# Moving the on-chip pools around layer 1's queries, keys and values, and context's values to the end, in a two-layer diffusion backbone

## The chip, the cores and the metric

One Trainium2 chip, one core of it. The metric is the device time of one execution in microseconds (us), for the whole kernel; the median of several runs counts. The kernel is written in Python against a tile framework that fixes, when the program is built, the order of the instructions in the queue of each engine: TensorE (PE, matmuls; PEld are its weight loads), VectorE (DVE), ScalarE (ACT), GpSimd (POOL) and SyncE (SP), from whose queue every transfer of this kernel is issued.

## What is computed

1024 latent tokens and 256 context tokens of 1024 channels go through two layers; the latent stream is the output. Layer 0 mixes with a recurrent block and a Fourier block, layer 1 with neighbourhood attention in which latent queries also read all context keys. Each layer ends with a gated feed-forward block, and every sub-layer is normalised, shifted, scaled and gated by vectors made from the conditioning (`w_mod`, `b_mod`). Cut to what matters here:

```python
for l in range(DEPTH):                      # DEPTH = 2
    mx = c_act @ w_mod[l] + b_mod[l]        # six vectors for latent tokens; mc: the same for context
    hx, hc = modulate(rmsnorm(x)), modulate(rmsnorm(ctx))
    yx, yc = _ab_mixer(hx, hc, ...) if l == 0 else _na_mixer(hx, hc, ...)
    x = x + gt1 * rmsnorm(yx)
    x = x + gt2 * rmsnorm((silu(fx @ wg) * (fx @ wu)) @ wd)     # fx = modulate(rmsnorm(x)), hidden 2816
    # layer 0 does the same for ctx

def _na_mixer(hx, hc, w_qkv, rpb, w_out, need_ctx):             # 16 heads of 64 channels
    q, k, v = split(hx @ w_qkv);  kc, vc = the same of hc @ w_qkv
    # each query: an 8 x 16 window of keys with a learned bias, and all 256 context keys, in one softmax
    o = softmax([q @ k_window + bias, q @ kc]) @ [v_window, vc]
    return o @ w_out
```

## The kernel before

All arithmetic is float32. TensorE works on pieces: a matrix is split into a high and a low part (ScalarE copies the high part, L326, VectorE subtracts for the low one, L327), and each product is three matmuls (L360, L361, L362). Most products of 512 by 512 blocks are done in a scheme with seven instead of eight block products; hence names as S1 to S4 for sums of weights, T1 to T4 for sums of input blocks, B11, B21, B22 for plain input blocks.

The stages in the order of the run: the mixer of layer 0 (to 345 us), its output product `out_proj0`, the feed-forward's first half `ffn_up` (to about 1060), its down product `ffn_down` (to about 1420), layer 1's values `values_of` (to about 1545), `queries_and_keys` (to 1728), `attention` (to 2008), its output product `out_proj1`, and layer 1's feed-forward (to the end).

**Memory.** Tiles come from pools. A pool is a stretch of the bytes of each partition, opened from the left end or from the right end as a stack, with a number of buffers for each name. Where a new pool lies over the bytes of a closed one, an instruction that writes the new pool is placed in its queue behind the last use of the whole old pool, so the layout decides how early a transfer can be issued. The pools that matter here: `raws` (weights as loaded), `units` (28 split pieces of 4 KB, both right), `hrow` (rows of the hidden layer, left, over ffn_up's pools), `y`, `x` and `v` (left), `uq` (the weights of queries and keys, left, over `v` with its two store buffers `vo`), `qt` (the buffers in which queries and keys are stored), `cxq` (context's split pieces, right), and attention's `q0`, `b0` (head 0's queries and bias, left, over `uq`), `k0` (head 0's keys, right, over `raws`), `qd`, `kd`, `bias`, `s`, `ot`, `vd`, `pt` (left).

**The down product.** `ffn_down` (L1207) goes over the hidden rows in two blocks: four latent token tiles and the context first, four latent tiles then. For each hidden row it loads down weights (L346), stored hidden values h (L1210, 512 KB for two rows) and for context c (L1216, 512 KB for four), splits them, and issues the matmuls. Between the rows it runs fillers: in block 0 the steps of layer 1's modulation vectors (`mod_steps_dve`, L435: VectorE multiplies and adds the loaded 256 KB weights, TensorE sums over the partitions), which end in `mod_finish` (L472). That adds the bias to the row (VectorE, L477), transposes it (four on TensorE, L480) and makes the gains. In block 1 the fillers make layer 1's input blocks.

**Values.** `values_of` (L1394) takes the weights in the order of `value_loads` (L1352). It begins with the context tokens' second half of the channels (g, 48 matmuls), then two passes r = 0, 1 with the blocks B11 and B21 and, between them, the context's first half; between the passes `tb.second` makes the rest of the input blocks; then the products T1, T2, B22, T3, T4. A result goes through `put` (L1406 ScalarE, L1407 VectorE, L1408 store) and two buffers `vo`.

**Queries and keys.** `queries_and_keys` runs over eight pairs of heads. `W.load` (L228) loads gate and up weights of a pair (rg, ru, 512 KB each), GpSimd makes the sums S1 to S4 (L198), the parts are split into ga, s1 to s4, up. Results are stored by a `put` of its own (L1477 to L1479), through two buffers `qo`.

**Attention.** For head 0, and one head ahead for the others, keys, queries, bias and every second head the values are loaded (L1577, L1578, L1581, L1582, L1585; the values 1.28 MB at once). Scores are matmuls (L1601, L1607), then a maximum with bias (VectorE, L1626), the exponential (ScalarE, L1632), a normalisation (GpSimd, L1640), transposes (L1656), and the product with the values (L1675).

Of the kernel before, what the change touches and what calls it, by code (L numbers as in the profile page):

```python
# [16 lines left out]
P = 128  # L17
# [13 lines left out]
ORDER = 'qd kd bias s ot vd pt'  # L31
# [65 lines left out]
class Blocks:  # L97
# [7 lines left out]
    def unit(self, name, k):  # L105
        u = self.u[name, k] = self.kern.unit()
        return u
# [67 lines left out]
class Weights:  # L175
# [3 lines left out]
    def __init__(self, kern, l, cx):  # L179
        self.kern, self.l, self.at, self.extra = kern, l, 0 if cx else 512, None  # L180

    def tile(self, tag, n, dt=F32R):
        return self.kern.t(self.kern.uw, [P, 2, n], dt, tag)
# [96 lines left out]
class Kernel:  # L280
# [136 lines left out]
    def mod_steps(self, l, g, pp, tag):  # L417
# [4 lines left out]
        def step(k):  # L422
# [7 lines left out]
            if k == KD - 1:  # L430
                self.mod_finish(l, g, ps, pp, tag)
# [3 lines left out]
    def mod_steps_dve(self, l, g, pp, tag, rows):  # L435
# [30 lines left out]
        def last():  # L466
            sum_up(3)
            self.mod_finish(l, g, st["ps"], pp, tag)

        return [lambda j=j, h=h: step(j, h) for j in range(4) for h in range(2)] + [last]  # L470

    def mod_finish(self, l, g, ps, pp, tag):  # L472
# [4 lines left out]
        nc.vector.tensor_tensor(mr, ps, bias, op=ALU.add)  # L477
        tp = self.t(pp, [P, 4, P], F32, tag)
# [577 lines left out]
    def open_main(self):  # L1056
# [3 lines left out]
        self.units = self.pool("units", bufs=NU, side="right", stack=self.u2)  # L1060

    def open_y(self, nx=0, side="left", ny=4):
# [4 lines left out]
        if nx:  # L1067
            xp = self.pool("x", bufs=nx, side=side, stack=st)
            self.xrow = lambda m: self.t(xp, [P, D], F32, "x")
        else:  # L1070
            self.xrow = lambda m: self.row()

# [134 lines left out]
    def ffn_down(self, l, blocks, hd, src, store, gg, fillers=((), ()), start=(0, 0), every=(1, 1), between=None):  # L1207
        def load(b, i):
            h = self.hunit().bitcast(F32) if b == 0 else self.unit().bitcast(F32)
# [3 lines left out]
        def loadc(i):  # L1213
            h = self.hunit("c", 2).bitcast(F32).rearrange("p q n -> p (q n)")
# [137 lines left out]
    def value_loads(self, unit, s1):  # L1352


        pool = self.nc.gpsimd.tensor_tensor
# [36 lines left out]
        return plain + sums + [lambda k=k: self.wload(src(1, 1, k), unit) for k in range(4)]  # L1392

    def values_of(self, vp, tb, rows, cx):  # L1394
# [5 lines left out]
        p5, p1 = ([self.t(vp, [P, 512], F32, f"{n}{i}") for i in range(4)] for n in ("q", "p"))  # L1400

        def put(m, half, c):
            u = self.t(vp, [P, 2, 512], F32R, "vo", bufs=2).rearrange("p q (z c) -> p (q z) c", c=P)
# [15 lines left out]
        g = banks("g", 2)  # L1419
        for k in range(KD):  # L1420
            mm(g, cx[k], self.ws.take(), k == 0, k == KD - 1)
        for i, m in enumerate(CTX):
            put(m, 1, g[i])
        g = banks("g", 2)
        for r in range(2):
            d = banks("d")
            for k in range(4):
                w = self.ws.take()
# [614 lines left out]
```

## Time and profile before

| | |
|---|---|
| median of three runs | 2784.2 us (2781.65 to 2784.48) |
| profiled execution | 2787.88 us |
| its span, first to last instruction | 2786.1 us |
| mean granted clock of TensorE | 0.973 of full speed |
| VectorE, ScalarE, GpSimd busy | 62%, 45%, 36% |
| moved by transfers | 397.5 MB, 143 GB/s over the span |

The span is what the profile shows, from the first to the last instruction; the profiled execution's own time is 1.8 us longer. In the rows further down a wait is read as "who <- releaser": the engine stood idle until the named instruction, or the landing of the named transfer, released it. "out<-in" are the names of the tiles written and read; "<-DMA" is a transfer. The clock is the share of full speed that TensorE was granted in a stretch, the DMA share the mean busy share of the core's 16 transfer engines. Matmuls overlap, so a matmul of 0.39 us is issued every 0.23 us at full clock.

### The profile page before, as it was taken

The numbers are of one execution on the slowest core, as the hardware profiler recorded it, in microseconds if no ns is written. First come the engines' busy times: TensorE is split into PE (matmuls) and PEld (weight loads), VectorE is DVE, ScalarE is ACT, GpSimd is POOL, SyncE is SP. The second block draws the span as 40 slices with busy tenths as digits, with TensorE's granted clock in tenths as the row PEclk, the third lists the DMA queues.
The fourth block names the chain that finished last, engine by engine and source line by source line (L and its number), as shares of the span: only waits on it lengthen the run. The fifth ranks groups of instructions, "written<-read, shape, count | busy, mean of one in ns | idle before, by whom it ended". The sixth has DMA issues, their size and how long they took to land. (4 is left out here: it accounts for less than half of the span.)

```text
span 2786.1 us, 36246 instructions
## 1 busy us (share of the span) xinstructions
PE 2607.2 (94%) x12770; PEld 2121.6 (76%) x12770; DVE 1715.0 (62%) x2568; ACT 1252.6 (45%) x2237; POOL 998.9 (36%) x868
## 2 busy tenths in 40 slices
PE   7999998899999998899988798899997999999997
PEld 3677577688888886677866686888875888888786
DVE  4665385856443435766567564777767666556966
ACT  3676254422223323334553342788855333333443
POOL 1000024444343430002036332677625555543811
PEclk9999999999999999999999899899999999999999
DMA  7333472233212226877435444877541332335634
GB/s 243 111 107 123 133 249 84 78 104 112 82 61 74 74 71 229 293 249 255 139 117 182 161 160 160 194 169 164 159 144 69 114 114 98 95 114 174 203 102 144
DMA packets 186664, 397.50 MB, mean 143 GB/s; under 512 B 19569, under 2 KB 49905, under 8 KB 184434
## 3 DMA queue, kind: packets, MB, share of 16 engines
q1 hardware_dynamic: 186482, 395.18, 44.3%
q8 instruction: 101, 1.65, 0.3%
q14 instruction: 81, 0.66, 0.1%
HBM read 309.65 MB, written 85.46 MB: 142 GB/s over the span
## 5 line engine op out<-in xcount | busy, mean ns | idle before, releaser
L360 PE MATMUL d<-u,u 128*128 128x512 f32 x768 | 303.8, 398 | 16.3 <-ACT u L326 10.1
L361 PE MATMUL d<-u,u 128*128 128x512 f32 x768 | 305.1, 397 | 5.2 <-DVE u L327 5.2
L362 PE MATMUL d<-u,u 128*128 128x512 f32 x768 | 303.6, 395 | 0.1
L326 ACT ACTIVATE u<-r 128x512 fp32r<-128x512 f32 x241 | 149.6, 627 | 254.4 <-DMA r<-in_w_down_dram 91.9
L327 DVE TENSOR_TENSOR s<-r,s 128x512 fp32r<-128x512 f32 x208 | 163.2, 792 | 155.2 <-ACT s L326 154.2
L260 POOL TENSOR_TENSOR ss<-ss 128x1 f32<-128x1 f32 x36 | 13.7, 380 | 678.1 <-ACT junk L258 677.9
L361 PE MATMUL g<-u,s 128*128 128x512 f32 x624 | 245.1, 393 | 5.1 <-POOL u L172 4.3
L327 DVE TENSOR_TENSOR u<-r,u 128x512 fp32r<-128x512 f32 x241 | 186.5, 781 | 102.5 <-ACT u L326 98.2
L360 PE MATMUL g<-u,s 128*128 128x512 f32 x624 | 244.5, 392 | 2.1 <-ACT u L122 1.9
L362 PE MATMUL g<-u,s 128*128 128x512 f32 x624 | 244.3, 392 | 0.0
L326 ACT ACTIVATE s<-r 128x512 fp32r<-128x512 f32 x208 | 127.3, 629 | 250.5 <-PE g L362 153.4
L198 POOL TENSOR_TENSOR r<-rg,ru 128x512 f32<-128x512 f32 x52 | 72.7, 1398 | 388.4 <-DMA rg<-in_w_gu_dram 132.4
L360 PEld LDWEIGHTS d<-u,u 128*128 128x128 f32 x768 | 146.4, 191 | 57.7 <-ACT u L326 15.2
L360 PE MATMUL d<-u,ga 128*128 128x512 f32 x416 | 165.7, 398 | 14.2 <-ACT ga L326 14.2
L1640 POOL TENSOR_TENSOR s<-s,sm 128x640 f32<-128x640 f32 (+1 forms) x128 | 151.0, 1200 | 77.7 <-DVE sm L1636 71.2
L361 PEld LDWEIGHTS d<-u,u 128*128 128x128 f32 x768 | 146.6, 191 | 38.8 <-DVE u L327 9.5
L362 PEld LDWEIGHTS d<-u,u 128*128 128x128 f32 x768 | 146.4, 191 | 31.3 <-DVE u L327 1.2
L362 PE MATMUL d<-u,ga 128*128 128x512 f32 x416 | 164.1, 395 | 0.7 <-DVE ga L327 0.6
L361 PE MATMUL d<-u,ga 128*128 128x512 f32 x416 | 164.3, 395 | 0.0
L1168 POOL TENSOR_TENSOR ub<-ub,ua 128x512 f32<-128x512 f32 x44 | 72.8, 1654 | 203.9 <-DVE ua L1167 197.0
L361 PEld LDWEIGHTS g<-u,s 128*128 128x128 f32 x624 | 118.1, 189 | 31.0 <-POOL u L172 5.6
L360 PEld LDWEIGHTS g<-u,s 128*128 128x128 f32 x624 | 117.9, 189 | 28.2 <-ACT u L122 3.5
(453 smaller groups left out, 7002.1 us busy)
## 6 DMA issues: line engine op xcount, KB each, us to landing
mraw<-in_w_mod_dram SPq DMA_DIRECT2D x192, 256.0 KB, 3.8
rg<-in_w_gu_dram SPq DMA_DIRECT2D x44, 512.0 KB, 4.1
ru<-in_w_gu_dram SPq DMA_DIRECT2D x44, 512.0 KB, 3.8
r<-in_w_down_dram SPq DMA_DIRECT2D x88, 256.0 KB, 4.3
x<-x SPq DMA_DIRECT2D x40, 512.0 KB, 4.6
qd<-qd SPq DMA_DIRECT2D x30, 512.0 KB, 11.1
r<-in_w_out_dram SPq DMA_DIRECT2D x48, 256.0 KB, 3.3
h<-hd SPq DMA_DIRECT2D x22, 512.0 KB, 6.3
```

Of the source, the lines that this page charges most:

```text
L198: pool(rs[3], rg[:, h1], ru[:, h1], op=ALU.subtract)
L260: nc.gpsimd.tensor_tensor(st, ss[:, 0:1], ss[:, 1:2], op=ALU.add)
L326: i = nc.scalar.activation(hi, src, AF.Copy) if eng == "act" else nc.vector.tensor_copy(hi, src)
L327: j = nc.vector.tensor_tensor(lo, src, hi.bitcast(F32), op=ALU.subtract)
L360: nc.tensor.matmul(ps, lhs[0], rhs[0], start=start, stop=False)
L361: nc.tensor.matmul(ps, lhs[0], rhs[1], start=False, stop=False)
L362: nc.tensor.matmul(ps, lhs[1], rhs[0], start=False, stop=stop)
L1168: pool(ub, ub, ua, op=add)
L1640: pin(nc.gpsimd.tensor_tensor(s, s, sm.to_broadcast([P, nl + L]), op=ALU.mult))
```

## The change

It lays pools elsewhere, splits one function and moves one piece of work.

- h and c rows of the down product come from `units`; `hrow` is gone. `units` has 20 buffers in layer 0, and 8 more, in a pool `early` to their right, are for the blocks B11 and B21 of layer 1 alone.
- `mod_finish` is split: `mod_row` adds the bias in the step in which it was, the rest is a filler step of its own (30 steps instead of 27; 10 of them in `ffn_up`, 20 in the down product).
- The gain rows get a pool `gg`; `x` is a pool of its own (6 buffers, 4 in block 1; 6 instead of 5 in layer 1's output product). `v` keeps s1, q and p; the store buffers `vo` are a pool on the right; the tiles of `values_of` that were `y` of `v` come from the `y` that stays.
- Context's first half of the values is computed at the end of `values_of`; its eight weight pieces are loaded and split once more.
- `up` of the queries and keys is a pool of its own above `uq`, so that `uq` (rg, ru, ga, s4, s1, s3, s2) lies over `y` and `v` only and `up` over `vo` and part of `v`.
- Attention: `kd`, `qd` and `bias` on the right, over `raws` and `early` only; head 0 uses them as every other head does; `s`, `ot`, `vd`, `pt` on the left, `vd` over `qt` and `cxq`.

```diff
...
-ORDER = 'qd kd bias s ot vd pt'
+ORDER = 'kd qd bias s ot vd pt'
+ASIDE = ("qd", "kd", "bias")
...
     def unit(self, name, k):
-        u = self.u[name, k] = self.kern.unit()
+        kern = self.kern
+        u = self.u[name, k] = kern.first_unit() if name in ("B11", "B21") else kern.unit()
...
     def turned(self, xs, k):
...
     def __init__(self, kern, l, cx):
-        self.kern, self.l, self.at, self.extra = kern, l, 0 if cx else 512, None
+        self.kern, self.l, self.at, self.extra, self.apart = kern, l, 0 if cx else 512, None, {}
     def tile(self, tag, n, dt=F32R):
-        return self.kern.t(self.kern.uw, [P, 2, n], dt, tag)
+        return self.kern.t(self.apart.get(tag, self.kern.uw), [P, 2, n], dt, tag)
     def load(self, f):
...
-                self.mod_finish(l, g, ps, pp, tag)
+                self.mod_finish(l, g, self.mod_row(l, g, ps), pp, tag)
...
         def last():
...
-            self.mod_finish(l, g, st["ps"], pp, tag)
-        return [lambda j=j, h=h: step(j, h) for j in range(4) for h in range(2)] + [last]
-    def mod_finish(self, l, g, ps, pp, tag):
+            st["mr"] = self.mod_row(l, g, st["ps"])
+        return ([lambda j=j, h=h: step(j, h) for j in range(4) for h in range(2)]
+                + [last, lambda: self.mod_finish(l, g, st["mr"], pp, tag)])
+    def mod_row(self, l, g, ps):
...
+        return mr
+    def mod_finish(self, l, g, mr, pp, tag):
+        nc, a = self.nc, self.a
...
-    def open_main(self):
+    def open_main(self, apart):
...
-        self.units = self.pool("units", bufs=NU, side="right", stack=self.u2)
+        self.first_unit = self.unit
+        if apart:
+            early = self.pool("early", bufs=8, side="right", stack=self.u2)
+            self.first_unit = lambda: self.t(early, [P, 2, 512], F32R, "u")
+        self.units = self.pool("units", bufs=NU - 8 * apart, side="right", stack=self.u2)
     def open_y(self, nx=0, side="left", ny=4):
...
-            xp = self.pool("x", bufs=nx, side=side, stack=st)
-            self.xrow = lambda m: self.t(xp, [P, D], F32, "x")
+            self.open_x(nx, side)
...
+    def open_x(self, n, side):
+        self.x_stack = ExitStack()
+        xp = self.pool("x", bufs=n, side=side, stack=self.x_stack)
+        self.xrow = lambda m: self.t(xp, [P, D], F32, "x")
     def load_scale(self, ms, src):
...
     def ffn_down(self, l, blocks, hd, src, store, gg, fillers=((), ()), start=(0, 0), every=(1, 1), between=None):
         def load(b, i):
-            h = self.hunit().bitcast(F32) if b == 0 else self.unit().bitcast(F32)
+            h = self.unit().bitcast(F32)
...
         def loadc(i):
-            h = self.hunit("c", 2).bitcast(F32).rearrange("p q n -> p (q n)")
+            h = self.row()
...
-        return plain + sums + [lambda k=k: self.wload(src(1, 1, k), unit) for k in range(4)]
+        last = [lambda r=r, c=c, k=k: self.wload(src(r, c, k), unit) for r, c in ((1, 1), (0, 0), (1, 0)) for k in range(4)]
+        return plain + sums + last
     def values_of(self, vp, tb, rows, cx):
...
-        p5, p1 = ([self.t(vp, [P, 512], F32, f"{n}{i}") for i in range(4)] for n in ("q", "p"))
+        p5, p1 = ([self.t(vp["v"], [P, 512], F32, f"{n}{i}") for i in range(4)] for n in ("q", "p"))
         def put(m, half, c):
-            u = self.t(vp, [P, 2, 512], F32R, "vo", bufs=2).rearrange("p q (z c) -> p (q z) c", c=P)
+            u = self.t(vp["o"], [P, 2, 512], F32R, "vo").rearrange("p q (z c) -> p (q z) c", c=P)
...
         def banks(tag, n=4):
...
-        g = banks("g", 2)
-        for k in range(KD):
-            mm(g, cx[k], self.ws.take(), k == 0, k == KD - 1)
-        for i, m in enumerate(CTX):
-            put(m, 1, g[i])
-        g = banks("g", 2)
+        def context(c):
+            g = banks("g", 2)
+            for k in range(KD):
+                mm(g, cx[k], self.ws.take(), k == 0, k == KD - 1)
+            for i, m in enumerate(CTX):
+                put(m, c, g[i])
+        context(1)
...
-                w = self.ws.take()
-                mm(d, tb.u[("B11", "B21")[r], k], w, k == 0, k == 3)
-                mm(g, cx[4 * r + k], w, r == 0 and k == 0, r == 1 and k == 3)
+                mm(d, tb.u[("B11", "B21")[r], k], self.ws.take(), k == 0, k == 3)
...
-            c = self.t(vp, [P, 512], F32, "y", bufs=self.ny)
+            c = self.t(self.yp, [P, 512], F32, "y", bufs=self.ny)
...
-        for i, m in enumerate(CTX):
-            put(m, 0, g[i])
         def product(tag, name):
...
-        u4 = [self.t(vp, [P, 512], F32, "y", bufs=self.ny) for _ in range(4)]
+        u4 = [self.t(self.yp, [P, 512], F32, "y", bufs=self.ny) for _ in range(4)]
...
+        context(0)
     def queries_and_keys(self, W, T, cx):
...
-        q0 = self.t(self.pool("q0", side="left", stack=self.kst), [P, 2, T], F32, "q0")
-        b0 = self.t(self.pool("b0", side="left", stack=self.kst), [P, 896], F32, "bi0")
-        k0p = self.pool("k0", side="right", stack=st)
-        be0 = self.t(k0p, [P, 512], F32, "be0")
-        k0 = self.t(k0p, [P, TT], F32, "k0")
...
-        pools = {n: self.pool(n, bufs=size.get(n, 1), side="left", stack=st) for n in ORDER.split()}
+        pools = {n: self.pool(n, bufs=size.get(n, 1), side="right" if n in ASIDE else "left", stack=st) for n in ORDER.split()}
...
-        bint = [b0, self.t(bp, [P, 896], F32, "bi1")]
-        bedge = [be0, self.t(bp, [P, 512], F32, "be1")]
+        bint = [self.t(bp, [P, 896], F32, f"bi{i}") for i in range(2)]
+        bedge = [self.t(bp, [P, 512], F32, f"be{e}") for e in range(2)]
...
-            kt = self.t(kd, [P, TT], F32, "kd") if h else k0
-            qt = self.t(qd, [P, 2, T], F32, "qd") if h else q0
+            kt = self.t(kd, [P, TT], F32, "kd")
+            qt = self.t(qd, [P, 2, T], F32, "qd")
...
-        self.open_main()
+        self.open_main(1)
...
-        self.ffn_up(0, W, tb, hd, cx, mods[:9])
+        self.ffn_up(0, W, tb, hd, cx, mods[:10])
...
-        self.open_y(6, ny=6)
+        self.open_y(0, ny=6)
+        gst = ExitStack()
+        gp = self.pool("gg", side="left", stack=gst)
+        self.open_x(6, "left")
...
-        gg = [self.gain_rows(0, 2, w, self.yp, self.pp, "g") for w in range(2)]
+        gg = [self.gain_rows(0, 2, w, gp, self.pp, "g") for w in range(2)]
...
-        hst = ExitStack()
-        hp = self.pool("hrow", side="left", stack=hst)
-        self.hunit = lambda tag="h", n=3: self.t(hp, [P, 2, 512], F32R, tag, n)
         def between():
-            hst.close()
...
+            self.x_stack.close()
+            self.open_x(4, "left")
...
+            vp["o"] = self.pool("vo", bufs=2, side="right", stack=vst)
         def vrow():
...
-                      (mods[9:], self.turn_steps(tb, rows, x2, cx, vp)), (0, TS), (2, 1), between)
+                      (mods[10:], self.turn_steps(tb, rows, x2, cx, vp)), (0, TS), (2, 1), between)
+        self.x_stack.close()
+        gst.close()
+        self.u_stack = ExitStack()
+        vp["v"] = self.pool("v", side="left", stack=self.u_stack)
+        vrow()
+        self.values_of(vp, tb, rows, cx)
+        self.u_stack.close()
...
-        self.u_stack = ExitStack()
-        vp["v"] = self.yp = self.pool("v", side="left", stack=self.u_stack)
-        vrow()
-        self.t(vp["v"], [P, 512], F32, "y", bufs=self.ny)
-        self.values_of(vp["v"], tb, rows, cx)
-        self.u_stack.close()
...
-        for n in "rg ru ga s4 s1 s3 s2 up".split():
-            self.t(self.uw, [P, 2048 if n in ("ga", "up") else 1024], F32, n)
+        for n in "rg ru ga s4 s1 s3 s2".split():
+            self.t(self.uw, [P, 2048 if n == "ga" else 1024], F32, n)
...
+        W.apart["up"] = self.pool("up", side="left", stack=self.u_stack)
...
-        self.open_main()
-        self.open_y(5, side="right")
+        self.open_main(0)
+        self.open_y(6, side="right")
...
+        self.x_stack.close()
...
```

The loads of a head in attention go in the order keys, queries, bias, values, as before; the arithmetic is the same, instruction for instruction, but for eight more splits of weight pieces.

## Rows read from the trace of the kernel before

**Rows 1.** The page, part 1: busy time of each engine over the span.
```profile
PE 2607.2 (94%) x12770; PEld 2121.6 (76%) x12770; DVE 1715.0 (62%) x2568; ACT 1252.6 (45%) x2237; POOL 998.9 (36%) x868
```

**Rows 2.** Waits of TensorE: in all, how often, the longest, us.
```profile
PE s L1601 <- DMA q<-qd: 16.3, 1, 16.3
...
PE d L360 <- ACT ga L326: 14.2, 1, 14.2
PE d L360 <- ACT u L326: 10.1, 2, 9.1
...
PE g L480 <- DVE mg L477: 7.5, 1, 7.5
```

**Rows 3.** Stretches: length, busy of PE, PEld, DVE, ACT, POOL; clock; DMA share, GB/s.
```profile
1071.00:1090.00 19.00, 19.00 (x78) 15.43 (x77) 13.51 (x26) 8.74 (x19) 0.00 (x0) 0.92 0.91 310
1090.00:1110.00 20.00, 20.00 (x86) 15.62 (x85) 14.89 (x27) 8.54 (x18) 0.00 (x0) 1.00 0.83 269
1148.00:1156.00 8.00, 0.55 (x3) 0.27 (x2) 5.87 (x12) 5.71 (x12) 0.00 (x0) 0.79 1.02 379
1156.00:1180.00 24.00, 24.00 (x101) 19.85 (x101) 17.30 (x33) 9.16 (x24) 0.00 (x0) 0.93 0.85 288
1457.00:1470.00 13.00, 8.08 (x37) 6.13 (x35) 12.73 (x11) 5.87 (x10) 10.92 (x8) 1.00 0.25 82
1535.00:1550.00 15.00, 1.04 (x2) 0.50 (x2) 5.54 (x8) 4.41 (x6) 0.78 (x1) 0.61 0.65 245
1745.00:1759.00 14.00, 10.68 (x49) 9.23 (x48) 6.83 (x19) 6.15 (x14) 5.07 (x5) 0.58 1.04 223
```

**Rows 4.** Time line, SyncE and ScalarE, after ffn_up: start, length, [idle before].
```profile
1062.46 3.50 SPq L1210 DMA_DIRECT2D h<-hd  x3
...
1069.67 0.63 ACT L326 ACTIVATE u<-h 128x512 fp32r<-128x512 f32 x1 [7.15 <-DMA h<-hd]
```

**Rows 5.** Time line, ScalarE and VectorE, in the down product.
```profile
1148.45 0.63 ACT L326 ACTIVATE u<-r 128x512 fp32r<-128x512 f32 x1 [4.46 <-DMA r<-in_w_down_dram]
...
1149.11 0.69 DVE L327 TENSOR_TENSOR u<-r,u 128x512 fp32r<-128x512 f32 x1 [3.41 <-ACT u L326]
...
1155.00 0.68 DVE L477 TENSOR_TENSOR mg<-g,mraw 128x512 f32<-128x512 f32 x1
```

**Rows 6.** Time line, SyncE, ScalarE and TensorE, from values to queries and keys.
```profile
1528.54 14.77 SPq L1408 DMA_DIRECT2D vd<-vo  x8
...
1547.85 1.06 ACT L326 ACTIVATE ga<-rg 128x1024 fp32r<-128x1024 f32 x1 [5.61 <-DMA rg<-in_w_qk_dram]
...
1548.96 0.80 PE L360 MATMUL d<-u,ga 128*128 128x512 f32 x1 [14.22 <-ACT ga L326]
```

**Rows 7.** Time line, SyncE, ScalarE and TensorE, from keys to attention.
```profile
1726.60 0.57 SPq L1585 DMA_DIRECT2D vd<-vd  x1
1728.03 3.42 SPq L1479 DMA_DIRECT2D kd<-qo  x2
...
1738.20 0.61 SPq L1578 DMA_DIRECT2D q<-qd  x1
...
1736.76 0.38 ACT L1477 ACTIVATE qo<-d 128x256 fp32r<-128x256 f32 x1 [6.58 <-DMA kd<-qo]
...
1744.31 0.77 PE L1601 MATMUL s<-k,q 128*128 128x256 f32 x2 [16.32 <-DMA q<-qd]
```

**Rows 8.** Attention by tile and line: ns min/median/max, first to last start.
```profile
L1577 SPq DMA_DIRECT2D k<-kd x2: 505/558/611, 1701.9 to 1707.0; - x2
...
L1675 PE MATMUL o<-pt,vd x704: 274/282/562, 1759.1 to 2007.5; 128*128 128x256 f32 x176
...
L1607 PE MATMUL s<-kd,qd x240: 278/280/416, 1761.2 to 1995.9; 128*128 128x256 f32 x120
```

**Rows 9.** The view of transfers: issues, KB each, median us to landing.
```profile
r<-in_w_out_dram SPq DMA_DIRECT2D x48, 256.0 KB, 3.3
...
vd<-vd SPq DMA_DIRECT2D x8, 1280.0 KB, 9.0
```

## The prediction

> **What bounds the kernel now.** I read the page first: TensorE is busy for 94% of the span [rows 1], so only time in which it stands still, or runs at the lower of its two clock levels, can be had back without less arithmetic; the change removes no arithmetic. Then the waits of TensorE [rows 2]; four long single ones lie where this change works: 16.3 us for the first queries of attention (wait G), 14.2 for the first gate weights of the queries and keys (F), 9.1 for the first split piece of the feed-forward's down product (C) and 7.5 for a modulation row inside it (D). Then the table of stretches [rows 3], for the clock behind each gap and for what else is near its limit. Last the time line around each gap, for what ended it [rows 4 to 7].
>
> C: the first three loads of stored hidden rows (h) are issued at 1062.46, and ScalarE, which splits them, gets the first at 1069.67 [rows 4]. In this kernel a load into a pool stands in SyncE's queue behind the last use of every pool that its own addresses overlap; h rows lie over ffn_up's pools. D: ScalarE gets the next row of down weights 4.46 us late, VectorE stands behind it in order, and so its addition of the modulation row starts at 1155.00 only, while TensorE has that row's transposes next in its queue [rows 5]. F: eight stores of values go out between 1528.54 and 1543.3, the gate weights' load stands behind them, and lands at 1547.85, 4.5 us after its issue; TensorE starts at 1548.96 after 14.22 us [rows 6]. G: head 0's key loads were issued while the keys were still made [rows 8], but its query loads wait for the pool uq and for the stores. A 1.28 MB load of attention's values enters at 1726.60 between those stores, such a load takes 9.0 us to land [rows 9], the store of 1728.03 holds its buffer until ScalarE can go on at 1736.76, the second query load leaves at 1738.20, and TensorE starts at 1744.31 [rows 7].
>
> The profiled execution took 2787.9 us, its span is 2786.1; the median of three runs is 2784.2, 3.7 lower. The sum is made against 2787.9 and the result lowered by the same 3.7. Runs of this kernel can tell 0.2%, 5.6 us, from no change.
>
> **Part 1, h and c rows from the units (C).** The pool hrow goes; its loads now need free units only, and units come free while ffn_up's last products run. So the loads can be issued some 15 us earlier, before its end, and ScalarE's 7.15 us of waiting [rows 4] ends ahead of TensorE's last product. Gain: the wait of 9.1 less 1 to 2 for what must still follow ffn_up's last output (x loads, gain rows), and part of the lower clock behind it: 0.92 over 19 us [rows 3] is 1.5 us lost. I take 9, ends 4 and 11. The price: weights, h and c rows and the first blocks of layer 1 now share 20 units and 8 early ones instead of 28 and a pool of their own; this lowers how far the splits run ahead. In 1090 to 1110 TensorE was busy for 20.00 of 20 us [rows 3]; I take 1 us of loss, ends 0 and 4 (more is rival 3).
>
> **Part 2, mod_finish split (D).** Its addition stays in its step, its four transposes come one filler step later, two hidden rows, some 8 us of matmuls. The addition was over at 1155.7, 7.4 us after TensorE stopped, so it is just in time; what is next in the queue, the products of the rows before, was split long before (only the transposes were waited for; after them 24.00 of 24 us are busy [rows 3]). Gain 7.5, plus a part of the clock (0.93 over 24 us, 1.7 lost): 8, ends 3 and 9, the lower one if ScalarE's late weights, which are what made VectorE late, show up as a wait further on. With the transposes move four copies, up to two small vector operations and, from the second group on, one load (the post-norm gains) on SyncE: all fall in slots where VectorE waited for ScalarE anyway [rows 5], 0. The three added filler steps fit in the slots of block 0.
>
> **Part 3, context's values last, and the pools v, vo, up (F).** The 48 context matmuls of one half, 11.2 us at 20.00/86 us each [rows 3], leave the two passes ahead of the second half of the input blocks and come after the last product. In 1457 to 1470 VectorE is the bound: 12.73 us of 13, TensorE 8.08 [rows 3]. Taking 24 matmuls, 5.6 us, out of the first pass lets VectorE's chain start 5.6 us earlier, and its two context splits of 0.7 us leave it: the last product ends 6.9 earlier. The 11.2 us of context then lie in the 14.22 us that TensorE waits anyway [rows 6], because the gate weights no longer lie over the store buffers: their load needs the last value's arithmetic, not its store. The stores still pace this arithmetic through two buffers, so the load goes out about 6.9 earlier, at 1536.4, lands 4.5 later, and split and start are as before: start at 1542, which is 7 earlier. Off this come 2 us for eight more weight loads of 256 KB (2.1 MB; in 1535 to 1550 the queues moved 245 GB/s at a share of 0.65, so the rest of their capacity, some 130 GB/s, would take it in 16 us: mostly hidden). A shorter gap gives 1 back in the clock. I take 6, ends 0 and 9. The splits of these weights (8 of 0.63 us on ScalarE, 0.69 on VectorE) lie in the time when VectorE is waited for; that is what the lower end holds. Context's two stores move behind all others on SyncE; nobody needs them before attention's values: 0.
> The Trainium skill (DMA: Bandwidth & Descriptors, Anatomy of one DMA) counts about 2 us fixed and the bytes at 436 GB/s for a transfer, fitted on another queue than SyncE's; for these 512 KB that makes an estimate of 3.2 us, where the row has 4.5. By the page the term would be 1.3 larger; the row decides.
>
> **Part 4, attention's pools (G).** kd, qd and bias now lie at the right over raws and the early units only, both done with the second product of the last pair, some 16 us before its end; nothing they load lies over uq. Queries and keys of head 0 are stored by then (its key loads left at 1701.9 and 1707.0 [rows 8]). So both pairs of loads go out near 1711 and land before TensorE's last product at 1728.0. The load of values lies over qt and cx and must now follow the last store, at about 1736 at the latest: it no longer stands between the stores. What remains: the scores follow the last product at once; their first softmax must wait until the splits of the last keys are through VectorE, about 1731.5 without the 6.58 us of ScalarE [rows 7]. The gain is 16.3 less 2 to 3 for this hand-over, plus up to 5.9 for a clock of 0.58 over 14 us [rows 3], of which I take 1 to 2, as a shorter gap also lowers the clock. Against it: the values' load, 9.0 us [rows 9], lands about 1745, and the first matmul with them, at 1759.1 [rows 8], would be due at 1744 to 1745: 0 to 2 lost. I take 15, ends 5 and 22.
>
> **Part 5, the rest.** raws now overlap kd, so the first rows of the output weights are loaded after the last scores at 1995.9 and not before; they land in 3.3 us [rows 9] and are needed at 2008, after twelve us of the last heads' values, which cover them: 0. If the queue were held until then, it would cost those 3.3. A sixth x buffer: 0, by the same cover. The mixer's end and out_proj0 have the same pools but for the cap on units: 0.
>
> **Sum:** 9 + 8 + 6 + 15 − 1 = 37. 2787.9 − 37 = 2750.9 for the execution, 2747 for the median.
>
> **Rivals.** (1) One of the two large waits stays: at F the stores, two at a time, remain what paces the end and the new loads take the queue from them, so F gives 0; or at G the loads are still placed behind the last stores and G gives 5. Then 31 or 27 us: about 2755 (2753 to 2757). For: SyncE issues everything in one order fixed ahead. Against: the only overlaps left are those named.
> (2) What C and D give back is waited for later, since the down product's block 0 is bound by transfers: share 0.83 to 0.85 in 1090 to 1110 and 1156 to 1180, and 1.02 in the gap D itself [rows 3]; the same bytes in 17 us less need a share of about 0.92. Then C and D give 0 to 4 of 17: 2747 + 15 = 2762. Against: TensorE misses nothing at 0.83 to 0.91.
> (3) Slower: the 20 units. Weights, split h, split c and their raw rows all come from one pool in block 0; if the lead falls under what a late load takes (4.46 us in D), TensorE waits at every filler step, some 20 of them. At 37/20 = 1.9 us each the gain is gone; at D's remaining size, 2.2 each, it is 44, and the time 2791. For: share 1.02 in 1148 to 1156. Against: live time per row is two hidden rows only, and 20.00 of 20 us with DMA at 0.83.
> (4) The change doesn't do what it says: a load remains behind an unnamed use (an overlap of v with y's last reader, of kd with a late raw): F and G both give half, C and D all: 2747 + 10 = 2757, inside rival 1's range; counted there.
>
> **Numbers.** Forecast 0.56, rival 1 with 4 0.22, rival 2 0.13, rival 3 0.09. The forecast's own range is 2734 (about all upper ends together, 11 + 9 + 9 + 22 = 51) to 2757, where rival 1 begins. The range to hold 8 of 10 reaches over rivals 1 and 2 with their bounds and leaves rival 3 and the far tail: 2734 to 2770. Faster by over 0.2%: forecast, 1 and most of 2: 0.88; within: rival 3 at about its point of balance, 0.05; slower 0.07.
>
> **What would show it.** C: no wait of TensorE above 2 us between 1055 and 1075, h loads issued before ffn_up's last product. D: no wait for L477's successor. F: context's matmuls after the last product, a wait of some 3 us for the gate weights in place of 14.2. G: loads of qd issued before the last key stores, TensorE's first scores within 2 us of its last product, the values' load last. Wrong: new waits of TensorE for u<-r or u<-h all through block 0, a wait for vd at the first values above 3 us, or a load of rg behind the last store.

## The result and the profile after

The changed kernel takes 2751.4 us in the median of four runs (2747.5 to 2757.0), the kernel before 2782.9 in the runs beside it: a ratio of 0.9892, interval 0.9868 to 0.9915. That is 31.5 us less, where the forecast was 37 (2747). A second measurement of the changed kernel gave 2748.4, ratio 0.9879 (0.9859 to 0.9898). The profiled execution has a span of 2751.6 us, 34.5 shorter than that of before.

The waits of TensorE in the changed kernel, columns as in [rows 2]:

```profile
PE s L1612 <- DVE mx L1637: 22.1, 9, 5.2
...
PE d L363 <- DVE u L329: 11.2, 7, 6.8
PE d L362 <- ACT u L328: 10.7, 2, 9.4
...
PE d L362 <- ACT ga L328: 2.5, 1, 2.5
```

The four waits of [rows 2] answer to this: G's 16.3 us for queries is gone, and the longest wait for a maximum (mx) is 5.2 instead; F's 14.2 is 2.5; C's and D's are gone; in D's place a wait of 3.3 us stands in the down product (below). The 9.4 for a split u looks like C's 9.1 but is another one: it lies in the values, and was not there before.

Where the time went is best read from lengths of stages, each from the first or last matmul of a name in the time line to the next such mark. They add up to TensorE's last matmul.

| us, from mark to mark | before | changed | changed, 2nd time |
|---|---|---|---|
| start to ffn_up's last | 1059.4 | 1059.9 | 1064.8 |
| to the down product's first (C) | 11.0 | 1.9 | 1.9 |
| to the values' first (D lies here) | 333.5 | 330.7 | 324.9 |
| to the first of queries and keys (F) | 145.1 | 140.0 | 141.3 |
| to their last | 179.0 | 178.3 | 178.3 |
| to the first with attention's values (G) | 31.1 | 18.0 | 17.0 |
| to the last of these | 248.7 | 244.2 | 247.0 |
| to TensorE's end | 765.6 | 765.7 | 765.7 |

The first row varies from 1052.7 to 1066.7 over the 14 traces kept here, and that of attention from 240.1 to 249.9. So a total tells no difference under some 5 us, and the experiments are read by the stage. The stages of C, F and G repeat within 1.5 us in the two traces of the changed kernel; the down product does not (330.7 and 324.9, at a clock of 0.98 and 1.00), and its length alone prices nothing under some 6 us.

Stretches of the changed kernel, columns as in [rows 3]:

```profile
1061.00:1071.00 10.00, 10.00 (x45) 7.70 (x42) 5.61 (x11) 6.56 (x14) 0.04 (x1) 1.00 1.00 307
...
1150.00:1166.00 16.00, 12.70 (x53) 10.13 (x52) 11.98 (x24) 6.58 (x18) 0.00 (x0) 0.91 0.96 349
...
1436.00:1457.00 21.00, 5.03 (x11) 3.54 (x12) 20.97 (x19) 10.51 (x18) 15.47 (x11) 0.59 0.21 62
...
1518.00:1533.00 15.00, 11.72 (x49) 8.98 (x49) 7.81 (x13) 6.79 (x11) 0.00 (x0) 0.99 0.84 289
```

The first is where C was: TensorE is busy for all of it, at full clock. The second is in the down product, behind the place of D: TensorE still stands for 3.30 us there, as its time line has it:

```profile
1164.04 0.80 PE L362 MATMUL d<-u,u 128*128 128x512 f32 x1 [3.30 <-DVE y L257]
```

The last is the end of the values, where it worked for 1.04 of 15 us before [rows 3] and now for 11.72, on context. The third is the price: in the second pass of the values TensorE has little to do for 21 us, while VectorE works for 20.97 of them.

The time line of the changed kernel, SyncE at C:

```profile
1044.78 0.63 SPq L1225 DMA_DIRECT2D u<-hd  x1
...
1046.14 1.19 SPq L1225 DMA_DIRECT2D u<-hd  x2
```

The h loads that left at 1062.46 [rows 4] leave 15 us before ffn_up's last matmul (1059.9).

SyncE, ScalarE and TensorE at F:

```profile
1525.50 0.32 SPq L1425 DMA_DIRECT2D vd<-vo  x1
1525.87 1.17 SPq L230 DMA_DIRECT2D rg<-in_w_qk_dram  x1
...
1531.32 1.06 ACT L328 ACTIVATE ga<-rg 128x1024 fp32r<-128x1024 f32 x1 [1.39 <-DMA rg<-in_w_qk_dram]
...
1532.43 0.50 PE L362 MATMUL d<-u,ga 128*128 128x512 f32 x1 [2.45 <-ACT ga L328]
```

The gate weights go out ahead of context's last two stores, not behind all of them as in [rows 6], and their landing lies under context's matmuls but for 2.45 us. The values began 11.4 us earlier; less this, the load leaves 6.1 earlier than before, where the forecast had 6.9.

SyncE, VectorE and TensorE at G:

```profile
1693.84 0.58 SPq L1588 DMA_DIRECT2D kd<-kd  x1
1694.51 0.55 SPq L1589 DMA_DIRECT2D qd<-qd  x1
...
1713.36 2.84 SPq L1495 DMA_DIRECT2D kd<-qo  x2
...
1719.55 0.57 SPq L1596 DMA_DIRECT2D vd<-vd  x1
...
1715.24 0.43 DVE L1494 SCALAR_TENSOR_TENSOR qo<-d,qo 128x256 fp32r<-128x256 f32 x1 [1.91 <-ACT qo L1493]
...
1710.60 0.40 PE L1612 MATMUL s<-kd,qd 128*128 128x256 f32 x2
...
1717.07 1.01 PE L1612 MATMUL s<-kd,qd 128*128 128x384 f32 x2 [5.24 <-DVE mx L1637]
```

The loads of head 0's keys and queries begin 17 us before the last product ends (1710.8); the first scores follow it at once; the values' load goes behind the last stores; and the first softmax waits until VectorE has split the last keys at 1715.24, which is the 5.24 us that stay.

### The profile page after: what moved, and what is told of

Its sections match the earlier page's. It is cut to its first block, busy times and chain, and to the rows that moved or that the text cites. A ratio compares the mean times of both kernels' runs of the same rounds, so it can differ in the third digit from the quotient of the medians.

```text
span 2751.6 us, 36277 instructions
## 1 busy us (share of the span) xinstructions
PE 2603.5 (95%) x12770; PEld 2120.1 (77%) x12770; DVE 1716.0 (62%) x2576; ACT 1257.5 (46%) x2245; POOL 990.2 (36%) x868
## 6 DMA issues: line engine op xcount, KB each, us to landing
qd<-qd SPq DMA_DIRECT2D x32, 512.0 KB, 10.6
```

## The experiments

Each but one is an edit of the changed kernel. Ratios are against the kernel before.

**1. C undone: h and c rows in a pool of their own again.**

```diff
-            h = self.unit().bitcast(F32)
+            h = (self.hunit() if b == 0 else self.unit()).bitcast(F32)
...
-            h = self.row()
+            h = self.hunit("c", 2).bitcast(F32).rearrange("p q n -> p (q n)")
...
+        hp = self.pool("hrow", side="left", stack=hst)
+        self.hunit = lambda tag="h", n=3: self.t(hp, [P, 2, 512], F32R, tag, n)
```

> The changed kernel with h and c rows back in a pool of their own over ffn_up's pools (units stay at 20 and 8). Theory: the place of that pool alone made the wait at the start of the down product, so TensorE's wait there is back at 8 to 9.5 us, and the rest of the stage is as in the changed kernel or 1 to 2 us better; total 6 to 9 us above the changed kernel, about 2759. Rival: the rows' share of the 20 units is what makes the 2.0 and 3.3 us waits left in the changed kernel's down product; then those two vanish and the total is 3 to 4 above it, about 2755.

Measured: 2763.0 us, ratio 0.9929 (0.9907 to 0.9951).

```profile
1065.75 3.08 SPq L1225 DMA_DIRECT2D h<-hd  x3
...
1072.51 0.63 ACT L328 ACTIVATE u<-h 128x512 fp32r<-128x512 f32 x1 [6.72 <-DMA h<-hd]
```

This is the time line of that kernel; it is [rows 4] again, and the stage of C is 10.6 us long against 1.9. The theory holds: the place of the pool made the wait. The rival falls: the down product behind it takes 331.3, not less than the 324.9 to 330.7 of the kernels whose rows share the units; it even has a wait of 6.14. The total lies 11.6 above the changed kernel, where 6 to 9 was expected; 8.7 of it is this stage, and the rest is within the spread of the others.

**2. D: the split of mod_finish, in three ways.** First undone in the changed kernel:

```diff
-            st["mr"] = self.mod_row(l, g, st["ps"])
+            self.mod_finish(l, g, self.mod_row(l, g, st["ps"]), pp, tag)
...
-                + [last, lambda: self.mod_finish(l, g, st["mr"], pp, tag)])
+                + [last])
```

> The changed kernel with mod_finish in one step again (27 filler steps, 9 of them in ffn_up). Theory: the addition of the modulation row stands behind splits that wait for late down weights, so TensorE's wait for the row is back at 5 to 8 us near 1140, but the lead that VectorE and ScalarE regain in it takes away the 3.3 us wait behind it: 2 to 4 us above the changed kernel, about 2754. Rival: the two waits have nothing to do with each other: 7 to 8 above, about 2759.

Measured: 2754.0 us, ratio 0.9893 (0.9869 to 0.9916). TensorE waits for the row again:

```profile
1142.41 1.12 PE L487 MATMUL g<-ident,mg 128*128 128x128 f32 x4 [6.71 <-DVE mg L480]
```

The 3.3 behind it is gone, and the down product takes 330.7 us, as in the first trace with the split. In the second trace with the split it takes 324.9, with waits of 1.5 and 1.0 only, so this run alone doesn't tell what the split is worth; the rival's 7 to 8 us above did not come. Then the split alone, in the kernel before:

> The kernel before with mod_finish split and nothing else. Theory: the wait of 7.5 us for the row goes, but the late down weights behind it then end in waits for split pieces of 4 to 8 us further on in the down product: within 3 us of the kernel before. Rival (the forecast's own step): nothing takes its place, 7 to 8 us below the kernel before.

Measured: 2784.2 us over ten runs, ratio 1.0003 (0.9986 to 1.0020). Its time line, TensorE, and ScalarE ahead of the second wait:

```profile
1153.77 0.66 PE L485 MATMUL g<-ident,mg 128*128 128x128 f32 x4 [1.22 <-DVE mg L478]
1173.01 0.79 PE L360 MATMUL d<-u,u 128*128 128x512 f32 x1 [6.33 <-DVE y L255]
...
1165.60 0.63 ACT L326 ACTIVATE u<-r 128x512 fp32r<-128x512 f32 x1 [6.31 <-DMA r<-in_w_down_dram]
```

The wait of 7.45 us for the row becomes 1.22 and a new one of 6.33, 19 us later. It is for L255, which reads out the banks of the first half of the product so that the second half can use them: ScalarE and VectorE come to it late, as they stand in order behind splits of down weights that land late (the load waited for left at 1158.85, behind modulation loads that took 4.70 and 2.13 us to issue, and took 6.7 us to land). The theory holds, with the place corrected: what came next was the read-out, not a split. Why the weights are late is seen on SyncE in the changed kernel:

```profile
1153.54 6.77 SPq L416 DMA_DIRECT2D mraw<-in_w_mod_dram  x3
1160.40 0.86 SPq L348 DMA_DIRECT2D r<-in_w_down_dram  x2
```

Three modulation loads take 6.77 us to issue, and down weights follow only at 1160.40. If it is a free buffer that the queue stands for (there are three), more buffers cure it:

```diff
-        self.open_mraw()
+        self.open_mraw(14)
```

> The changed kernel with 14 buffers instead of 3 for loaded modulation weights in the down product (in the bytes that the h and c rows left). Theory: the waits of 2.0 and 3.3 us left there come from SyncE's queue, which stands for a buffer of these weights with down weights behind; they vanish, and the values start 4 to 6 us earlier: about 2747. Rival: the transfers themselves are the bound (share 0.85 to 0.96): the loads then come earlier and take the same share, the waits move and stay within 1.5 us of their sum, about 2751; or the loads, ahead of the down weights, make them later: up to 5 us more.

Measured: 2741.5 us, ratio 0.9850 (0.9818 to 0.9881). Stretches of that kernel:

```profile
1066.00:1085.00 19.00, 19.00 (x82) 14.77 (x82) 16.21 (x28) 7.61 (x16) 0.00 (x0) 1.00 1.05 390
...
1145.00:1165.00 20.00, 20.00 (x89) 16.44 (x88) 16.08 (x28) 11.42 (x27) 0.00 (x0) 1.00 0.94 321
```

TensorE is busy throughout both, with shares of 1.05 and 0.94 and 390 GB/s at the highest, and the down product takes 323.5 us. What SyncE's queue stood for between 1065 and 1240 us, columns as in [rows 2], first in the changed kernel:

```profile
SPq L416 <- DMA mraw<-in_w_mod_dram: 40.1, 22, 4.0
```

Then with 14 buffers:

```profile
SPq L416 <- DMA mraw<-in_w_mod_dram: 2.6, 8, 0.3
```

So in the changed kernel the transfers were not the bound; one queue was, which stood for three buffers. With these buffers, and mod_finish in one step:

> The changed kernel with 14 buffers and mod_finish in one step again. Theory: what makes the modulation row late is SyncE's queue standing for a buffer with down weights behind it; with 14 buffers the weights are on time, TensorE waits under 2 us for the row, and the total is within 2 us of the run with 14 buffers and the split. Rival: the addition is late because it stands in order behind splits on VectorE whatever the loads do: a wait of 5 to 7 us, and as much above.

Measured: 2740.1 us, ratio 0.9848 (0.9827 to 0.9869); the down product takes 320.4 us and TensorE has no wait over 0.6 us in block 0. With the buffers the split is worth nothing to be seen: the theory.

**3. F: order and pools apart.** First context's half back in the two passes, pools as changed:

```diff
-                mm(d, tb.u[("B11", "B21")[r], k], self.ws.take(), k == 0, k == 3)
+                w = self.ws.take()
+                mm(d, tb.u[("B11", "B21")[r], k], w, k == 0, k == 3)
+                mm(g, cx[4 * r + k], w, r == 0 and k == 0, r == 1 and k == 3)
...
-        context(0)
```

> The changed kernel with context's half of the values back in the two passes (no extra weight loads), pools as changed. Theory: the pools alone let the gate weights' load go before the last stores, but nothing lies over its landing: the last product ends about 5 us later than in the changed kernel and a wait of 5 to 9 us stands before the first product of queries and keys; total 4 to 7 above the changed kernel, about 2757. Rival: the order does nothing, as the passes are bound by VectorE: the total is within 1.5 us of the changed kernel.

Measured: 2757.5 us, ratio 0.9911 (0.9883 to 0.9939).

```profile
1524.22 0.42 SPq L230 DMA_DIRECT2D rg<-in_w_qk_dram  x1
...
1530.51 0.80 PE L362 MATMUL d<-u,ga 128*128 128x512 f32 x1 [11.37 <-ACT ga L328]
```

The stage of the values takes 143.7 us: of the 5.1 that the changed kernel gains over 145.1 (3.8 in its second trace), the pools alone give 1.4. The theory's total came out, but by chance: the stage is 2.4 to 3.7 longer than in the changed kernel, the wait is 11.37 and not 5 to 9, and attention took 249.9 us, the longest of all. The rival falls by the stage. Then the order alone, by laying `up` back into uq, which so lies over the values' store buffers:

```diff
-        for n in "rg ru ga s4 s1 s3 s2".split():
+        for n in "rg ru ga s4 s1 s3 s2 up".split():
...
-        W.apart["up"] = self.pool("up", side="left", stack=self.u_stack)
```

> The changed kernel with up back in the pool uq, which then lies over the store buffers of the values (attention's pools stay on the right). Theory: attention needs only one of the two moves, so its gap stays at 5 to 7 us (first wait), but the first gate weights stand behind the last store of values, context's stores included: 8 to 12 us more before the first product of queries and keys; total 8 to 12 above the changed kernel, about 2761. Rival: up apart is what lets attention start, whatever its pools: then a wait of 14 to 17 us before its scores as well, about 2772.

Measured: 2751.4 us, ratio 0.9877 (0.9855 to 0.9900). TensorE before queries and keys, and at the second group of scores in attention:

```profile
1529.31 0.80 PE L362 MATMUL d<-u,ga 128*128 128x512 f32 x1 [8.62 <-ACT ga L328]
...
1714.89 1.01 PE L1612 MATMUL s<-kd,qd 128*128 128x384 f32 x2 [5.50 <-DVE mx L1637]
```

The wait before the first product of queries and keys is 8.62 us instead of 2.45, and the stage takes 146.4, no less than before the change. Neither half gives the gain; both together do. (The expected loss of 8 to 12 was 5 to 6 in the stage; the total doesn't show it, the spread of the other stages being as large.) In attention its first wait is 5.50 us, as in the changed kernel.

**4. G: attention's pools undone.**

```diff
+        q0 = self.t(self.pool("q0", side="left", stack=self.kst), [P, 2, T], F32, "q0")
...
-        pools = {n: self.pool(n, bufs=size.get(n, 1), side="right" if n in ASIDE else "left", stack=st) for n in ORDER.split()}
+        pools = {n: self.pool(n, bufs=size.get(n, 1), side="left", stack=st) for n in ORDER.split()}
...
-            kt = self.t(kd, [P, TT], F32, "kd")
-            qt = self.t(qd, [P, 2, T], F32, "qd")
+            kt = self.t(kd, [P, TT], F32, "kd") if h else k0
+            qt = self.t(qd, [P, 2, T], F32, "qd") if h else q0
```

> The changed kernel with attention's pools as before the change (head 0's queries and bias on the left over the queries' and keys' weights, its keys on the right, kd, qd and bias on the left; x with 5 buffers in the output product after it). Theory: the wait of 16 us before the first scores is back, with the load of values between the last stores: 16 to 18 above the changed kernel, about 2768. Rival: most of the gap was the hand-over of the last keys through two store buffers and the softmax, so 8 to 11 above, about 2761.

Measured: 2754.2 us, ratio 0.9897 (0.9873 to 0.9921). Both expectations fall: the first wait is 6.20 us, and the stage of G takes 21.4 against 31.1 before and 18.0 changed. So the layout of attention is worth 3.4 of 13.1, given the rest of the change. A new theory: in this kernel head 0's queries lie over uq again, as before the change; what matters is which work ends last in uq, and with `up` gone from it that work ends before the last two products, which read `up`. Then undoing both must bring the wait back, and `up` alone must not (that was experiment 3's second kernel).

> The changed kernel with both undone: attention's pools as before the change and up in uq. Theory: with the queries of head 0 over a pool that ends with the last product again, the 14 to 17 us before the first scores are back, with the 8 to 12 us before queries and keys: 18 to 28 above the changed kernel, about 2774. Rival: the gap of the kernel before came from the order of the load of values alone, which follows the stores now: a first wait of 6 to 8 us and 10 to 14 above, about 2763.

Measured: 2763.3 us, ratio 0.9920 (0.9898 to 0.9941). The time line of TensorE at the start of attention, first with attention's pools alone undone:

```profile
1715.41 0.77 PE L1617 MATMUL s<-k,q 128*128 128x256 f32 x2 [6.20 <-issue]
```

Then with both undone:

```profile
1723.54 0.77 PE L1617 MATMUL s<-k,q 128*128 128x256 f32 x2 [16.16 <-DMA q<-qd]
```

First waits of 5.24 (neither undone), 5.50 (`up`), 6.20 (attention) and 16.16 (both): either move suffices, and the two don't add. SyncE's queue, again first with attention's pools alone undone:

```profile
1695.84 0.61 SPq L1594 DMA_DIRECT2D q<-qd  x1
...
1709.81 0.61 SPq L1594 DMA_DIRECT2D q<-qd  x1
...
1714.73 0.57 SPq L1601 DMA_DIRECT2D vd<-vd  x1
```

Then with both undone:

```profile
1705.97 0.57 SPq L1601 DMA_DIRECT2D vd<-vd  x1
...
1710.88 0.72 SPq L1594 DMA_DIRECT2D q<-qd  x1
...
1717.99 0.61 SPq L1594 DMA_DIRECT2D q<-qd  x1
```

With both undone the first load of queries leaves 3.5 us after the last product (1707.4) and not 13.4 before it (1709.2), which is what the new theory asks for. But the theory is not the whole of it. With attention's pools alone undone, the first load at 1695.84 left 7.8 us before the last product that reads uq was over (1703.6); so the pool decides the place in SyncE's queue at most, and what sets that place was not followed up. And with both undone the load of values has moved as well, from behind the last stores to between them, as in [rows 7], and the second load of queries leaves only behind the last store of keys (1717.42). So no run here tells the place of the queries from the place of the values, and the rival, whose load of values was to follow the stores, was not put to the test. The total was 11 nearer to the changed kernel than the theory had it; the rival's total came out, by other stages.

**5. A better version.** Beside the 14 buffers, the second pass's weight splits ahead of the input blocks, and a store buffer for the last keys:

```diff
+                self.ws.finish(self.ws.at + 4)
                 tb.second(rows)
...
+            u = self.t(tp, [P, 2, L], F32R, "qc") if n == L else self.t(tp, [P, 2, 512], F32R, "qo", bufs=2)
```

> The 14 buffers, and two more edits of the changed kernel: the four weight splits of the values' second pass are issued before the rest of the input blocks is made, and the last keys (of context) have a store buffer of their own. Theory: T1 starts 2 to 3 us earlier, since that split no longer stands behind the input blocks on ScalarE and VectorE, and attention's first softmax 2 us earlier; with 4 to 6 of the buffers 8 to 11 below the changed kernel, about 2742. Rival: VectorE is busy throughout the stretch before T1, so the place of one split changes nothing there (under 1 us), and the softmax has its next wait in the bias: 4 to 6 below, about 2747.

Measured: 2746.3 us, ratio 0.9858 (0.9837 to 0.9879): the rival's total, and its reason for the values. The waits in the values move behind the pass (8.8 and 6.2 us), since VectorE is the bound there, and the stage takes 138.4 us against 138.7; the first softmax comes 2 us earlier, and the first matmul with attention's values doesn't: 17.7 us against 17.8. Here the rival's reason, the bias, is not what the trace shows:

```profile
1714.05 1.43 PE L1687 MATMUL o<-pt,vd 128*128 128x256 f32 x10 [2.34 <-DMA vd<-vd]
```

That matmul waits for the landing of the values, whose load leaves 8.8 us after the last product (8.1 with the 14 buffers alone); VectorE's wait of 5.33 for a bias comes 4 us later.

> The changed kernel itself once more, so that the runs beside it have it on the same chip: 2748 to 2755 by either theory.

> The changed kernel with 14 buffers for loaded modulation weights and the early split of the second pass's weights, without the store buffer for the last keys. Theory: the buffers give the 5 to 8 us in the down product that their first run showed, and the early split 1 to 2 before queries and keys: 6 to 10 below the changed kernel of this call. Rival: the first run of the buffers was a good draw of attention, whose length differs by up to 10 us between runs of the same code: 3 to 4 below it.

Measured: the changed kernel 2748.4 us (2745.5 to 2755.6); with the buffers and the early split 2742.2, ratio 0.9855 (0.9832 to 0.9879). That is 6.2 below, at the theory's lower edge. The three kernels with 14 buffers but without the store buffer lie at 2740.1 to 2742.2, 6 to 11 under the two measurements of the changed kernel. Their intervals still overlap or touch it; the down product does not: 320.4 to 323.9 us in four traces with them, 324.9 to 331.3 in eight of the changed kernel and its other variants. They are faster than the kernel before, and by that stage and the queue's waits than the changed one, by an amount that the totals leave open; the early split adds nothing to be seen.

## Why the prediction was right, and where it was not

**C, 9 forecast:** 9.1 (11.0 to 1.9) in both traces. The mechanism and the size were as written; the price of 1 us for 20 units did not show.

**D, 8 forecast: the step that failed.** "What is next in the queue ... was split long before" was true, and the wait for the row went. But the cause, ScalarE's late weights, stayed, and in the kernel before 6.3 of 7.45 us came back at the read-out of the first half (3.3 in the changed kernel); alone the split is worth 0 (ratio 1.0003, where 8 us less would be 0.9971). The lower end of 3, "if ScalarE's late weights ... show up as a wait further on", named the mechanism and still put it too high. Rival 2 had the waits move too, but by transfers at their limit; with the queue no longer held up, the same bytes went without a wait at shares of 0.94 and 1.05. Still the down product is 2.8 to 8.6 us shorter in the changed kernel than before, and is 2.8 shorter without the split; what gives this (the clock, which was 0.98 and 1.00 in its two traces and 0.98 before, the first rows' earlier start, or the pools) was not taken apart.

**F, 6 forecast:** 5.1 and 3.8. The load left within 1 us of the time worked out. That the second pass would then wait 16 us for a split behind the input blocks was not foreseen; it costs little because VectorE's work, not TensorE's, sets that stretch. The page named there makes the landing, by estimate, 3.2 us where the row had 4.5 (the Trainium skill, DMA: Bandwidth & Descriptors, Anatomy of one DMA); in the changed kernel it was 5.5 (1525.87 to 1531.32), in a stretch with a DMA share of 0.84 where before it was 0.65 [rows 3]. The measurement is further off the page's figure than before.

**G, 15 forecast:** 13.1 and 14.1 to the first matmul with attention's values, the rest within the spread of attention. The end was right: scores at once, the softmax after the last split (1715.2, forecast 1731.5 less the 17 that came before). The cause was only one of two: "nothing they load lies over uq" is enough, but so is `up` taken out of uq, which the forecast counted for F alone.

**The sum:** 9.1 + 2.8 + 5.1 + 0.7 + 13.1 + 4.5, less 0.5 in the first row, is 34.8 between the trace before and the first of the changed kernel, and the medians have 31.5. Forecast 37; in these two traces D's 2.8 for 8 makes most of the difference. In the second trace the down product is 8.6 shorter and the first row, where nothing was meant to change, 5.4 longer, so that D's share of the total can't be read from two traces; that its step failed is read from the split alone in the kernel before. Rival 1 fell by F and G, rival 3 by the down product's length.

## What to carry to other kernels

Where a pool may be written only behind all of an older pool's work, ask which tile of the older pool is used last: one tile moved out let the loads over the others leave earlier here. A wait that is ended by an engine which itself waited is not cured by giving its waiter other work; follow the releaser back until a queue or a resource comes, here one in-order queue that stood for three buffers. And fill a gap at the end of a stage only together with what starts the next one: the layout gave 1.4 alone and the order nothing, and together they gave 5.1 and 3.8.

## What was not expected of the hardware

VectorE took 0.68 us for the subtraction of L174 when GpSimd was idle, and 1.7 beside GpSimd's work, in the stretch that bounds the values. The time line of the changed kernel, VectorE:

```profile
1434.28 5.12 DVE L174 TENSOR_TENSOR u<-y,u 128x512 fp32r<-128x512 f32 x3
...
1453.91 0.68 DVE L174 TENSOR_TENSOR u<-y,u 128x512 fp32r<-128x512 f32 x1
```

GpSimd, idle for 1.16 us around the second row:

```profile
1454.60 1.73 POOL L1388 TENSOR_TENSOR s<-r,r 128x512 f32<-128x512 f32 x1 [1.16 <-DVE u L174]
```

GpSimd was busy for 15.47 of the 21 us there. The Trainium skill (SBUF — State Buffer, SBUF: two separate sides) says that the two share a port pair which one of them holds for a whole instruction; the rows agree, and no run here took the work off GpSimd. The other surprise is the spread: attention took 240 to 250 us in kernels with the same code for it. Its longest and its shortest, in the kernel of experiment 3 with the order undone and in the one with 14 buffers, columns as in [rows 3]:

```profile
1725.70:1975.60 249.90, 232.55 (x1778) 223.11 (x1777) 194.82 (x493) 220.21 (x497) 190.72 (x187) 0.96 0.72 167
...
1718.60:1958.70 240.10, 226.65 (x1778) 217.26 (x1776) 193.78 (x492) 219.96 (x496) 190.65 (x187) 0.99 0.74 174
```

VectorE's waits there for one bias tile (a single buffer, loaded again for each head) were 15.9 and 15.6 us in all, so they don't make the 10 us; the granted clock was 0.96 and 0.99. Whether the clock makes the length or other waits make both was not tried.
